# Hybrid encoder layer: the pooling products folded into the output weights on the chip, one pair of gates computed among the quads, and the weight sums begun later

## The chip, the cores and the metric

The kernel runs on one core of a Trainium2 chip. The metric is the device time of one execution in microseconds (us). The kernel before takes 2693.46 us (median of three runs, 2693.1 to 2695.12). Five engines work side by side: TensorE (PE) multiplies, VectorE (DVE) and ScalarE (ACT) do elementwise work, GpSimd (POOL) and SyncE (SP) here mainly issue transfers. Each executes its own instructions in program order and waits for the others by semaphores.

## The reference

One encoder layer on two requests of 256 and 1024 tokens (1280 in all), with 1024 channels, all in float32. What matters here is the mixing part:

```
z = rmsnorm(x) @ w_in                       # rq rk rv rg pin mq gl
gates = sigmoid(gl)                          # 3 x 1024 channels
# pooling branch, group gi of 256 channels, window w = 2, 4, 8, 16
mean = (cs[hi] - cs[lo]) / (hi - lo)         # centred window
d[gi] = mean - pin[gi]
y = einsum('bsgc,gcd->bsgd', d, pool_w) * pool_scale
y_pool = y @ w_pool_out
merged = gates[0]*y_ret + gates[1]*y_pool + gates[2]*y_mem
x = x + rmsnorm(merged @ w_o)
```

The other two branches are retention and attention over 256 memory tokens for each request, and a GeGLU network with 2 x 2816 inner columns follows. Between the differences `d` and `y_pool` there are only products with constants, so `pool_w`, `pool_scale` and `w_pool_out` can be multiplied with each other first.

## The kernel before

A float32 product is made of three matmuls (`mm3`, L161): each operand is split into a rounded high part and a low part, and high x high, high x low and low x high are added up. The high part is an ACT copy, the low part a DVE subtraction (`hilo`, L152; for weights `Weights.split`, L89 and L90). So every operand costs ACT and DVE time before PE can use it.

Weights come as units of 128 x 1024 (512 KB) in one fixed order. `Weights` keeps two raw tiles (`wr`, loaded by SP) and four split pairs (`wh`, `wl`). `take` hands units out and splits the next ones as soon as a pair is free; a load waits until the split of the unit two places before has freed its raw tile. A *gate unit* is one weight unit against all 1280 tokens: 24 matmuls for each of two groups of 512 tokens and one of 256, each followed by a sigmoid on ACT and a store by POOL.

`tick()` (L310) stands between groups of matmuls. It lets the weight ring take a step, issues `adding[0]` steps of the *weight sums*, and then advances each generator in the background list `bg` to its next `yield`. That is how the order of the work is set: nothing is rescheduled, the program order of the generators is the order on each engine.

The weight sums (`sums`, L201) are sums of weight quarters made by accumulating transfers of POOL through DRAM (five steps per pair of units: two copies on ACT's queue, then L214, L216, L218 and L220 on POOL's). They feed the *quads* (L611 on): a Strassen-like form for two weight units, in which 1024 of the tokens cost 84 matmuls of 512 columns in place of 96; the other 256 tokens take 48 matmuls of 256 columns in either form. The quads make `mq`, `pin` and `rg`, 12 in all, and take 229 to 527 us.

The stages of the first third are: memory keys and values (to 117 us; the values' group is `mem_v`, L523, and beside it x, loaded by POOL as `xr`, is normalised in the background, `x_stats`), the V projection (to 229), the quads, the memory stage (to 727), the pool stage (to about 915), the state and retention stages, and the merge that multiplies the three branches with their output weights.

In the memory stage PE multiplies K's rotary units (`rotary_unit`, L843 on) while `mem_chain` (L781 on) runs in the background: it loads K and V of a head, splits them (`khl`, `vhl`), and makes scores, softmax and outputs for 40 jobs. It yields three times before the first `split_k`. One gate unit follows.

In the pool stage PE multiplies nine gate units while two generators run. `pool_chain` (L901) takes the eight half groups m = 0 to 7 (two `pin` tiles, loaded by SP). For each it adds shifted copies on DVE (L939, L944; one add for window 2, four for window 16), mends the edges (L952, L955), forms the difference (L959), splits it on ACT and DVE (`dh`), and after two of them multiplies them with the split `pool_w` of the group (`pwh`) and stores the result (`ypo` on ACT, `yp_d`). `decay_matrix` (L461) makes four tables `dtab` for the retention: two DVE instructions for each (L467, L468), then a table load and four exponentials on ACT (L472), then four masks on DVE (L475).

Of the kernel before, what the change touches and what calls it, by code (L numbers as in the profile page):

```python
# [59 lines left out]
class Weights:  # L60
# [33 lines left out]
    def tick(self):  # L94
        self.load()
        self.split()
# [28 lines left out]
def encoder(ctx: ExitStack, tc: tile.TileContext, a: dict):  # L125
# [55 lines left out]
    def rsqrt_act(pool, v, between=None):  # L181
# [4 lines left out]
        if between:  # L186
# [9 lines left out]
             for k, o in (("mq", 40), ("pin", 32), ("rg", 24)) for i in range(H)]  # L196
# [46 lines left out]
    N_MEM, N_POOL = 1, 9  # L243
# [6 lines left out]
    gates = [w_in[48 + i] for i in range(24)]  # L250
    srcs += [w_in[8 + i] for i in range(8)] + gates[:N_MEM + N_POOL]
    srcs += [w_in[i] for i in range(8)] + gates[N_MEM + N_POOL:]
    srcs += [a["w_mem_out"][i] for i in range(8)]
    srcs += [a["w_pool_out"][i] for i in range(8)]
# [49 lines left out]
    def sum_step(n=1):  # L304
        for _ in range(n):
            next(summing, None)
# [194 lines left out]
    with tc.tile_pool(name="st0", bufs=2) as stp:  # L501
# [121 lines left out]
    with tc.tile_pool(name="quads", bufs=1) as qp:  # L623
# [25 lines left out]
        def emit(q, e, o, n, src, t=None):  # L649
            kind, i = quads[q][:2]  # L650
            if kind == "rg":
                y = t or qtile()
                s = qtile()
                nc.scalar.activation(s[:, 0:n], src, AF.Sigmoid)
                nc.vector.scalar_tensor_tensor(out=y[:, 0:n], in0=src, scalar=col("ret_gn", 2 * i + e), in1=s[:, 0:n],
                                               op0=ALU.mult, op1=ALU.mult)
                dst = g_d
            else:
                y = t
                if t is None:  # L660
                    y = qtile()
                    snap(y[:, 0:n], src)
                dst = mq_d if kind == "mq" else pin_d
            nc.gpsimd.dma_start(out=dst[i][:, e, o:o + n], in_=y[:, 0:n])
# [64 lines left out]
    def mem_chain():  # L729
# [83 lines left out]
        yield  # L813
        yield
        yield
# [49 lines left out]
    gate_n = [0]  # L865
# [36 lines left out]
    def pool_chain():  # L902
        pieces = ((PAD, 0, TP), (PAD + TP + PAD, TP, TS))
        pin = [pp.tile([P, PWA], F32, name=f"pin{i}") for i in range(2)]
        for t in pin:
            for s in (0, PAD + TP, PW - PAD):
                nc.gpsimd.memset(t[:, s:s + PAD], 0.0)

        def load(m):
            if m < 2 * len(WINDOWS):  # L910
                t = pin[m % 2]
                for s, o, n in pieces:
                    nc.sync.dma_start(out=t[:, s:s + n], in_=pin_d[m // 2][:, m % 2, o:o + n])

        load(0)
        load(1)

        def load_w(g):
            if g < len(WINDOWS):
                t = pwr[g] = pp.tile([P, 2, HD], F32, tag="pwr", name="pwr")  # L920
                nc.sync.dma_start(out=t, in_=a["pool_w"][:, g])

        pwr = {}
        load_w(0)
        yield
        for g, w in enumerate(WINDOWS):
            ph = pp.tile([P, 2, 2, HD], F32R, tag="pwh", name="pwh")
            hilo(pwr.pop(g)[:], ph[:, 0], ph[:, 1])
            load_w(g + 1)
            dh = []  # L930
            for c in range(2):
                x = pin[c]
                cur, lo, hi = x, PAD - 8, PW - PAD + 7
                step = 1
                while step < w:
                    t = pp.tile([P, PWA], F32, tag=f"ps{step in (2, 8)}", name="ps")
                    if step == 1:
                        lo += 1
                        nc.vector.tensor_tensor(out=t[:, lo:hi], in0=cur[:, lo - 1:hi - 1], in1=cur[:, lo:hi],  # L939
                                                op=ALU.add)  # L940
                    else:
                        k = step // 2
                        lo, hi = lo + k, hi - k
                        nc.vector.tensor_tensor(out=t[:, lo:hi], in0=cur[:, lo - k:hi - k],  # L944
                                                in1=cur[:, lo + k:hi + k], op=ALU.add)
                    cur = t
                    step *= 2
                    if step == 8:
                        yield
                for s, _, n in pieces:  # L950
                    e0 = cur[:, s:s + w // 2]
                    nc.vector.tensor_tensor(out=e0, in0=e0, in1=kcol(f"s{w}"), op=ALU.mult)  # L952
                    if w > 2:
                        e1 = cur[:, s + n - w // 2 + 1:s + n]
                        nc.vector.tensor_tensor(out=e1, in0=e1, in1=kcol(f"e{w}"), op=ALU.mult)  # L955
                    else:
                        e1 = cur[:, s + n - w // 2:s + n]
                r = cur[:, PAD:PW - PAD]
                nc.vector.scalar_tensor_tensor(out=r, in0=r, scalar=1.0 / w, in1=x[:, PAD:PW - PAD],  # L959
                                               op0=ALU.mult, op1=ALU.subtract)  # L960
                t = pp.tile([P, 2, PWA], F32R, tag="dh", name="dh", bufs=2)[:, :, 0:PCOLS]
                hilo(r, t[:, 0], t[:, 1])
                dh.append(t)
                yield
                load(2 * g + c + 2)
            yield
            for e in range(2):
                es = slice(e * P, (e + 1) * P)
                for s, o, n in ((0, 0, TP), (TP + PAD, TP, 512), (TP + PAD + 512, TP + 512, 512)):
                    b = chb(n)  # L970
                    for c in range(2):
# [5 lines left out]
                yield  # L977

    bg.append(pool_chain())
    bg.append(decay_matrix(pp))  # L980
    for _ in range(N_POOL):
        gate_unit(pp)
# [904 lines left out]
def _prepare(i, np):  # L1887
# [23 lines left out]
        "w_pool_out": _unit_fm(i["w_pool_out"][0], np),  # L1911
# [4 lines left out]
        "pool_w": i["pool_w"][0].reshape(4, 2, P, HD).transpose(2, 0, 1, 3),  # L1916
# [38 lines left out]
```

## Time and profile before

| what | value |
|---|---|
| median of three runs | 2693.46 us |
| the profiled execution, its span | 2693.02 us, 2691.0 us |
| PE busy | 2620.8 us, 97% |
| DVE, ACT, POOL busy | 53%, 36%, 12% |
| PE clock granted, mean | 0.986 |

PE is the engine that does nearly all of the span, so a stage gets shorter either by fewer matmul columns or by fewer waits of PE. A clock of 1.0 is 2.4 GHz; a stretch at half of it (1.2 GHz) shows as a clock below 1.0 in a window. A busy time of matmuls is modelled and each overlaps its neighbours, so the cost of one is read from the distance of two starts.

### The profile page before, as it was taken

What the parts mean: (1) busy time and instruction counts of PE and PEld (TensorE: products, weight loads), DVE (VectorE), ACT (ScalarE), POOL (GpSimd) and SP (SyncE); (2) the same over time, 40 slices, a digit from 0 to 9 for tenths busy, and PEclk for the clock granted to TensorE, in tenths of its full rate; (3) what the DMA queues carried; (4) which work ended last, traced back from release to release, by engine and by line L of the source; (5) the groups of instructions that cost most, each with busy time, mean ns of one, the idle gap of its engine ahead of it and who ended that gap; (6) DMA issues with size and microseconds to landing.
All of it is one profiled execution on the core that took longest, in us unless ns stands there. A gap on an engine that the chain in (4) does not pass through costs nothing.

```text
span 2691.0 us, 35137 instructions
## 1 busy us (share of the span) xinstructions
PE 2620.8 (97%) x13580; PEld 2240.8 (83%) x13580; DVE 1414.4 (53%) x2343; ACT 974.7 (36%) x1631; POOL 335.4 (12%) x507
## 2 busy tenths in 40 slices
PE   8899999999979899999999999998999999999998
PEld 6688888889958788888888888877888888888887
DVE  4542223466443465788633453557655666664554
ACT  5322223334332242333321120566444444444443
POOL 1111222212222222111100000010000000000000
PEclk9899999999989999999999999998999999999999
DMA  7986888877667787755344343453333333354443
GB/s 266 309 232 179 229 241 228 243 216 217 164 186 199 201 254 190 222 179 198 134 162 134 115 155 102 147 178 94 118 108 116 111 110 109 113 186 153 144 159 109
DMA packets 181429, 464.86 MB, mean 173 GB/s; under 512 B 20720, under 2 KB 48240, under 8 KB 180720
## 3 DMA queue, kind: packets, MB, share of 16 engines
q1 hardware_dynamic: 111072, 268.33, 30.3%
q0 software_dynamic: 54384, 146.83, 21.1%
q10 hardware_dynamic: 15808, 47.47, 5.5%
q8 instruction: 106, 1.74, 0.3%
q14 instruction: 59, 0.48, 0.1%
HBM read 360.58 MB, written 182.19 MB: 202 GB/s over the span
## 4 chain that ended last, share of the span: by engine, by line
PE 80%; issue 7%; DVE 5%; DMA 4%; ACT 2%; POOL 1%; SPq 0%; DVEq 0%; ACTq 0%; POOLq 0%
PE f L1521 15%; PE f L164 10%; PE f L163 9%; PE f L162 9%; PE mm L637 7%; PE mm L162 6%; PE mm L163 6%; PE mm L164 6%; PE ch L163 3%; PE ch L164 3%; PE ch L162 3%; PE ch L637 1%; DMA ypd<-ypo 1%; DVE ps L944 1%; DMA qkvr<-vd 1%
## 5 line engine op out<-in xcount | busy, mean ns | idle before, releaser
L90 DVE TENSOR_TENSOR wl<-wr,wh 128x1024 fp32r<-128x1024 f32 x268 | 327.4, 1223 | 493.7 <-ACT wh L89 488.7
L89 ACT ACTIVATE wh<-wr 128x1024 fp32r<-128x1024 f32 x268 | 280.7, 1051 | 282.0 <-PE f L163 156.5
L162 PE MATMUL mm<-b,wh 128*128 128x512 f32 (+1 forms) x960 | 342.8, 357 | 1.3 <-DVE rt L858 1.3
L163 PE MATMUL mm<-b,wh 128*128 128x512 f32 (+1 forms) x960 | 340.9, 355 | 0.0
L164 PE MATMUL mm<-b,wl 128*128 128x512 f32 (+1 forms) x960 | 340.5, 355 | 0.0
L1521 PE MATMUL f<-b,wh 128*128 128x512 f32 x880 | 274.4, 393 | 0.0
L162 PEld LDWEIGHTS mm<-b,wh 128*128 128x128 f32 x960 | 182.5, 190 | 25.8 <-DVE rt L858 1.8
L164 PEld LDWEIGHTS mm<-b,wl 128*128 128x128 f32 x960 | 182.1, 190 | 25.8
L163 PEld LDWEIGHTS mm<-b,wh 128*128 128x128 f32 x960 | 182.4, 190 | 23.6
L1521 PEld LDWEIGHTS f<-b,wh 128*128 128x128 f32 x880 | 162.3, 190 | 30.8
L1521 PE MATMUL f<-b,wl 128*128 128x512 f32 x440 | 172.0, 391 | 0.0
L163 PE MATMUL f<-b,wh 128*128 128x512 f32 (+1 forms) x432 | 153.4, 355 | 0.0
L162 PE MATMUL f<-b,wh 128*128 128x512 f32 (+1 forms) x432 | 153.2, 355 | 0.0
L164 PE MATMUL f<-b,wl 128*128 128x512 f32 (+1 forms) x432 | 152.8, 354 | 0.0
L164 PE MATMUL f<-wh,gl 128*128 128x512 f32 x390 | 151.8, 389 | 0.1
L162 PE MATMUL f<-wh,gl 128*128 128x512 f32 x390 | 151.7, 389 | 0.0
L163 PE MATMUL f<-wl,gl 128*128 128x512 f32 x390 | 151.7, 389 | 0.0
L155 DVE TENSOR_TENSOR gl<-b,gl 128x640 fp32r<-128x640 f32 x78 | 64.2, 824 | 118.3 <-ACT gl L154 118.2
L637 PE MATMUL mm<-T,wh 128*128 128x512 f32 x384 | 118.7, 391 | 0.0
L154 ACT ACTIVATE gl<-b 128x640 fp32r<-128x640 f32 x78 | 57.5, 740 | 153.7 <-PE f L164 153.7
L1521 PE MATMUL f<-hc,wh 128*128 128x512 f32 x352 | 108.9, 391 | 0.0
L162 PE MATMUL f<-h2p,wh 128*128 128x256 f32 x352 | 100.4, 285 | 3.2 <-ACT h2p L154 3.2
(383 smaller groups left out, 5919.6 us busy)
## 6 DMA issues: line engine op xcount, KB each, us to landing
wr<-w_in_in SPq DMA_DIRECT2D x72, 512.0 KB, 5.9
wr<-w_up_in SPq DMA_DIRECT2D x44, 512.0 KB, 3.5
wr<-w_down_in SPq DMA_DIRECT2D x44, 512.0 KB, 3.5
wr<-s12d SPq DMA_DIRECT2D x34, 512.0 KB, 3.6
wr<-s34d SPq DMA_DIRECT2D x34, 512.0 KB, 3.6
b<-fgd SPq DMA_DIRECT2D x44, 320.0 KB, 5.1
h2s<-gtd SPq DMA_DIRECT2D x48, 256.0 KB, 3.8
s12d<-w_up_in ACTq DMA_DIRECT2D x22, 512.0 KB, 5.8
```

Of the source, the lines that this page charges most:

```text
L89: self.nc.scalar.activation(h, r[:], AF.Copy)
L90: self.nc.vector.tensor_tensor(out=l, in0=r[:], in1=h.bitcast(F32), op=ALU.subtract)
L154: nc.scalar.activation(hi, src, AF.Copy)
L155: nc.vector.tensor_tensor(out=lo, in0=src, in1=hi.bitcast(F32), op=ALU.subtract)
L162: nc.tensor.matmul(out, ah, bh, start=first, stop=False)
L163: nc.tensor.matmul(out, ah, bl, start=False, stop=False)
L164: nc.tensor.matmul(out, al, bh, start=False, stop=last)
L637: nc.tensor.matmul(b, w[x][:, ks], in_term(nm, c, y), start=first and c == k == 0, stop=last and c == 3 and k == 2, skip_group_check=True)
L944: nc.vector.tensor_tensor(out=t[:, lo:hi], in0=cur[:, lo - k:hi - k], in1=cur[:, lo + k:hi + k], op=ALU.add)
L1521: nc.tensor.matmul(b, w[x][:, ks], hterm(nm, c, y), start=first and c == k == 0, stop=last and c == 3 and k == 2, skip_group_check=True)
```

## The change

It has five parts.

1. The quads get a thirteenth kind `gate`, made of gate units 0 and 1 (`NG = 2`); `emit` applies the sigmoid and writes to `gate_d`.
2. The memory stage has two gate units in place of one, and the pool stage 2 + 1 + 2 + 1 = 6 in place of 9. With the two in the quads the number before the state stage stays ten.
3. `pool_chain` no longer splits the differences nor multiplies: POOL stores them to `yp_d` as they are. In their place `fold(g)` multiplies the transposed `pool_w` of group g, scaled by `pool_scale` in its split (`fold_split`), with two weight units of `w_pool_out` from the ring: four blocks of 512 columns, each of two products of three matmuls, so 24 matmuls. The result goes to DRAM (`wp_d`) by ACT and POOL and is read as the merge's pooling weights. `pool_wT` (1 MB) comes in one load on SP. `decay_matrix` is now ahead of `pool_chain` in `bg`.
4. In `tick` the sums' step comes after the background generators, and `adding[0] = 1` is set when the first `mem_v` runs, three ticks later than before. There are 35 sums in place of 34.
5. `mem_chain` yields four times in place of three before `split_k(0)`.

```
-             for k, o in (("mq", 40), ("pin", 32), ("rg", 24)) for i in range(H)]
+             for k, o in (("mq", 40), ("pin", 32), ("rg", 24)) for i in range(H)] + [("gate", 0, w_in[48], w_in[49])]
-    N_MEM, N_POOL = 1, 9
+    NG, N_MEM, N_FOLD = 2, 2, (2, 1, 2, 1)
...
+    gates = [w_in[48 + i] for i in range(NG, 24)]
+    wp_d = dram.tile([P, KC, KC, P], F32, name="wpd")
+    srcs += [w_in[8 + i] for i in range(8)] + gates[:N_MEM]
+    gates = gates[N_MEM:]
+    for g in range(len(WINDOWS)):
+        srcs += [a["w_pool_out"][2 * g], a["w_pool_out"][2 * g + 1]] + gates[:N_FOLD[g]]
+        gates = gates[N_FOLD[g]:]
-    srcs += [a["w_pool_out"][i] for i in range(8)]
+    srcs += [wp_d[:, i].rearrange("p a b -> p (a b)") for i in range(KC)]
...
     def tick(step=True):
         ws.tick()
-        sum_step(adding[0])
         for g in list(bg) if step else ():
...
+        sum_step(adding[0])
...
         def mem_v(p, j, b):
+            adding[0] = 1
...
-        adding[0] = 1
         token_major(8, memT, 4, mem_v)
...
+            elif kind == "gate":
+                y = t or qtile()
+                nc.scalar.activation(y[:, 0:n], src, AF.Sigmoid)
+                dst = gate_d[2 * i + e]
...
-        yield
-        yield
-        yield
+        for _ in range(4):
+            yield
         split_k(0)
...
-                t = pp.tile([P, 2, PWA], F32R, tag="dh", name="dh", bufs=2)[:, :, 0:PCOLS]
-                hilo(r, t[:, 0], t[:, 1])
...
-            for e in range(2):
-                es = slice(e * P, (e + 1) * P)
-                for s, o, n in ((0, 0, TP), (TP + PAD, TP, 512), (TP + PAD + 512, TP + 512, 512)):
-                    b = chb(n)
-                    for c in range(2):
-                        mm3(b, ph[:, 0, c, es], ph[:, 1, c, es], dh[c][:, 0, s:s + n], dh[c][:, 1, s:s + n],
-                            c == 0, c == 1)
-                    y = pp.tile([P, 512], F32, tag="ypo", name="ypo", bufs=2)
-                    nc.scalar.activation(y[:, 0:n], b, AF.Copy, scale=col("pool_scale", 2 * g + e))
-                    nc.gpsimd.dma_start(out=yp_d[g][:, e, o:o + n], in_=y[:, 0:n])
+            for s, o, n in pieces:
+                nc.gpsimd.dma_start(out=yp_d[m // 2][:, m % 2, o:o + n], in_=cur[:, s:s + n])
             yield
+            load(m + 2)
+    bg.append(decay_matrix(pp))
     bg.append(pool_chain())
-    bg.append(decay_matrix(pp))
-    for _ in range(N_POOL):
-        gate_unit(pp)
+    pwr = pp.tile([P, 4, 2, HD], F32, name="pwr")
+    nc.sync.dma_start(out=pwr, in_=a["pool_wT"])
+    pw = pp.tile([P, 2, 4, 2, HD], F32R, name="pw")
+    def fold_split(g):
+        for d in range(2):
+            hilo(pwr[:, g, d], pw[:, 0, g, d], pw[:, 1, g, d], col("pool_scale", 2 * g + d))
+    def fold(g):
+        rows = ws.take(2)
+        for c in range(2):
+            cs = slice(c * P, (c + 1) * P)
+            for f in range(2):
+                b = chb(512)
+                fs = slice(f * 512, (f + 1) * 512)
+                for d in range(2):
+                    mm3(b, pw[:, 0, g, d, cs], pw[:, 1, g, d, cs], rows[d][0][:, fs], rows[d][1][:, fs],
+                        d == 0, d == 1)
+                o = pp.tile([P, 512], F32, tag="wpo", name="wpo", bufs=4)
+                nc.scalar.activation(o, b, AF.Copy)
+                nc.gpsimd.dma_start(out=wp_d[:, 4 * f:4 * f + 4, 2 * g + c, :],
+                                    in_=o[:].rearrange("p (a b) -> p a b", b=P))
+    for g in range(len(WINDOWS)):
+        fold_split(g)
+        fold(g)
+        tick()
+        for _ in range(N_FOLD[g]):
+            gate_unit(pp)
```

On DVE, just before the second product group of the pool stage, the kernel before has the following (`pwh` is the low part of that group's `pool_w`, `wl` that of a weight unit, the last two rows are the first adds of half group m = 2):

```order
L468 SCALAR_TENSOR_TENSOR dtab<-rel,lg,dtab 128x512
L90 TENSOR_TENSOR wl<-wr,wh 128x1024
L155 TENSOR_TENSOR pwh<-pwr,pwh 128x512
L939 TENSOR_TENSOR ps<-pin_6191 128x1310
L944 TENSOR_TENSOR ps<-ps 128x1308
```

and the changed kernel, just before the second fold (`pw` is the low part of the second group's `pool_w`; the first row is the difference of m = 3, the three adds are those of m = 4):

```order
L952 SCALAR_TENSOR_TENSOR ps<-ps,pin_6500 128x1296
L480 TENSOR_SCALAR dtab<-dtab 128x512 x4
L934 TENSOR_TENSOR ps<-pin_6499 128x1310
L939 TENSOR_TENSOR ps<-ps 128x1308
L939 TENSOR_TENSOR ps<-ps 128x1304
L158 SCALAR_TENSOR_TENSOR pw<-pwr,pk,pw 128x256 x2
L90 TENSOR_TENSOR wl<-wr,wh 128x1024
```

Before, `pwh` stood ahead of its group's adds, and the differences of m = 2 and m = 3 behind it were what the products waited for; now no product needs a difference, but `pw` stands behind m = 2, m = 3, the four masks of `dtab` and the adds of m = 4. On ACT the exponentials of `dtab` with a table load on either side stand in both kernels in the last gate unit ahead of this place; now the copy of the second `pool_w` is the next but one after them.

At the start of the memory stage DVE has, in the kernel before (`khl`, `qhl` and `vhl` are the low parts of the memory's keys, queries and values, `rot` a rotated K, `mx` the first maximum of the softmax):

```order
L860 TENSOR_TENSOR rot<-rt_4306,rt_4307 128x2x256
L155 TENSOR_TENSOR khl<-kraw,khl 128x1024
L155 TENSOR_TENSOR qhl<-qraw,qhl 128x512
L155 TENSOR_TENSOR vhl<-vraw,vhl 128x1024
L777 TENSOR_REDUCE mx<-ch 128x2
```

and in the changed one, with the third group (256 columns) of the rotary unit in between:

```order
L868 TENSOR_TENSOR rot<-rt_4500,rt_4501 128x2x256
L155 TENSOR_TENSOR khl<-kraw,khl 128x1024
L155 TENSOR_TENSOR qhl<-qraw,qhl 128x512
L866 TENSOR_TENSOR rt_4573<-mm,cos 128x256
L867 TENSOR_TENSOR rt_4574<-mm,sin 128x256
L868 TENSOR_TENSOR rot<-rt_4573,rt_4574 128x256
L866 TENSOR_TENSOR rt_4573<-mm,sin 128x256
L867 TENSOR_TENSOR rt_4574<-mm,cos 128x256
L868 TENSOR_TENSOR rot<-rt_4573,rt_4574 128x256
L155 TENSOR_TENSOR vhl<-vraw,vhl 128x1024
L786 TENSOR_REDUCE mx<-ch 128x2
```

The keys' split keeps its place behind the same rotation, while the first maximum, and so the first scores on PE, come one group of matmuls later.

POOL's loads of the transposed input `xT`, which is normalised in the background of the memory values, stand among the first sums before:

```order
L371 DMA xr<-xT_in 128x1280 x5
L214 DMA s12d_71<-w_in_in 256x1x512
L371 DMA xr<-xT_in 128x1280 x2
L214 DMA s12d_72<-w_in_in 256x1x512
L371 DMA xr<-xT_in 128x1280
L216 DMA s34d_105<-w_in_in 128x512
```

and ahead of all of them after:

```order
L376 DMA xr<-xT_in 128x1280 x8
L214 DMA s12d_71<-w_in_in 256x1x512
L214 DMA s12d_72<-w_in_in 256x1x512
L216 DMA s34d_106<-w_in_in 128x512
L214 DMA s12d_73<-w_in_in 256x1x512
```

No load of `xT` is now behind a sum.

## Rows read from the trace of the kernel before

**Rows 1.** The page's busy time of each engine, share and instructions, whole span.

```profile
PE 2620.8 (97%) x13580; PEld 2240.8 (83%) x13580; DVE 1414.4 (53%) x2343; ACT 974.7 (36%) x1631; POOL 335.4 (12%) x507
```

**Rows 2.** Busy us by stretch: start:end, length, engines, granted clock, DMA share, GB/s.

```profile
230.00:530.00 300.00, 300.00 (x1592) 259.35 (x1591) 96.92 (x107) 91.81 (x133) 84.07 (x118) 1.00 0.84 228
530.00:570.00 40.00, 35.25 (x178) 30.38 (x177) 18.81 (x32) 8.62 (x16) 8.38 (x11) 0.91 0.92 254
...
752.00:908.00 156.00, 128.47 (x625) 108.07 (x626) 71.75 (x84) 47.92 (x71) 43.03 (x65) 0.89 0.68 178
```

**Rows 3.** Chain of waits in a quad: start, us, what.

```profile
240.07 0.12 PE ch L162
...
241.50 5.47 PE mm L637 x24
```

**Rows 4.** Waits of PE, pool stage (724 to 908): us, times, longest.

```profile
PE ch L162 <- ACT dh L154: 22.6, 5, 7.4
PE ch L163 <- DVE dh L155: 5.1, 5, 1.2
```

**Rows 5.** Busy us by stretch around the second wait of the pool stage.

```profile
758.00:765.00 7.00, 2.19 (x6) 1.71 (x7) 5.50 (x8) 3.67 (x5) 2.42 (x4) 0.50 0.41 68
765.00:772.00 7.00, 7.00 (x39) 6.13 (x38) 2.95 (x5) 0.81 (x2) 1.68 (x3) 0.77 0.95 257
```

**Rows 6.** Groups by line and form, pool stage: busy, mean ns | idle before.

```profile
L90 DVE TENSOR_TENSOR wl<-wr,wh 128x1024 fp32r<-128x1024 f32 x9 | 11.0, 1222 | 67.6 <-ACT wh L89 67.6
...
L975 ACT ACTIVATE ypo<-ch,pk 128x512 f32<-128x512 f32 x15 | 10.3, 688 | 46.0 <-DMA ypd<-ypo 38.6 <-PE ch L164 7.3
L869 ACT ACTIVATE gate<-mm 128x512 f32<-128x512 f32 x17 | 10.0, 591 | 14.4 <-PE mm L164 13.7 <-ACT wh L89 0.6
L89 ACT ACTIVATE wh<-wr 128x1024 fp32r<-128x1024 f32 x9 | 9.5, 1053 | 0.0
...
L468 DVE SCALAR_TENSOR_TENSOR dtab<-rel,lg,dtab 128x512 f32<-128x512 f32 x4 | 3.0, 751 | 0.1
...
L467 DVE TENSOR_SCALAR dtab<-rel,lg 128x512 f32<-128x512 f32 x4 | 2.0, 488 | 0.0
L475 DVE TENSOR_SCALAR dtab<-dtab 128x512 f32<-128x512 f32 x4 | 1.4, 417 | 0.0
```

**Rows 7.** DVE's timeline, first and last instruction of one half group, window 4.

```profile
788.53 1.52 DVE L939 TENSOR_TENSOR ps<-pin 128x1310 f32<-128x1310 f32 x1
...
792.04 1.51 DVE L959 SCALAR_TENSOR_TENSOR ps<-ps,pin 128x1296 f32<-128x1296 f32 x1
```

**Rows 8.** ACT's timeline at the decay tables' exponentials.

```profile
780.41 1.28 ACT L472 ACT_TABLE_LOAD   x1
781.70 2.19 ACT L472 ACTIVATE dtab<-dtab 128x512 f32<-128x512 f32 x4
```

**Rows 9.** Landing of the tiles pin, then pwr (min/median/max), whole span.

```profile
DMA to landing us min/median/max: 2.1/5.3/7.9
DMA to landing us min/median/max: 3.0/5.8/8.7
```

**Rows 10.** DMA issues of the pool stage: the table of distances.

```profile
rel<-rel_in SPq DMA_DIRECT2D x1, 512.0 KB, 10.4
```

**Rows 11.** Waits of PE, 60 to 130 us.

```profile
PE mm L162 <- ACT sv L525: 9.8, 2, 5.3
```

**Rows 12.** Chain of waits from 100 to 118 us.

```profile
100.93 12.59 DMA xr<-xT_in
```

**Rows 13.** DVE's timeline at that load's landing.

```profile
113.54 1.49 DVE L415 TENSOR_TENSOR xr<-xr,xrb 128x1280 f32<-128x1280 f32 x1 [2.71 <-DMA xr<-xT_in]
```

**Rows 14.** Waits of PE, 530 to 570 us.

```profile
PE ch L163 <- DVE khl L155: 3.4, 1, 3.4
```

**Rows 15.** DVE's timeline at the end of that wait.

```profile
556.01 1.22 DVE L155 TENSOR_TENSOR khl<-kraw,khl 128x1024 fp32r<-128x1024 f32 x1
```

More of the change, by code (lines that the diff above doesn't have):

```diff
@@ L662, in emit @@
                     snap(y[:, 0:n], src)
-                dst = mq_d if kind == "mq" else pin_d
-            nc.gpsimd.dma_start(out=dst[i][:, e, o:o + n], in_=y[:, 0:n])
+                dst = (mq_d if kind == "mq" else pin_d)[i][:, e]
+            nc.gpsimd.dma_start(out=dst[:, o:o + n], in_=y[:, 0:n])
         def close(q, e, o, op, x, y):
@@ L863, in rotary_unit @@
             tick()
-    gate_n = [0]
+    gate_n = [NG]
     def gate_out(m, pool, o, n, b):
@@ L909, in load @@
         def load(m):
-            if m < 2 * len(WINDOWS):
-                t = pin[m % 2]
+            if m < KC:
                 for s, o, n in pieces:
-                    nc.sync.dma_start(out=t[:, s:s + n], in_=pin_d[m // 2][:, m % 2, o:o + n])
+                    nc.sync.dma_start(out=pin[m % 2][:, s:s + n], in_=pin_d[m // 2][:, m % 2, o:o + n])
         load(0)
         load(1)
[L918 to L921, printed above, removed]
@@ L979, in encoder @@
-    bg.append(pool_chain())
-    bg.append(decay_matrix(pp))
-    for _ in range(N_POOL):
-        gate_unit(pp)
+        yield
+        yield
+        for m in range(KC):
+            w, x = WINDOWS[m // 2], pin[m % 2]
+            cur, lo, hi = x, PAD - 8, PW - PAD + 7
+            step = 1
+            while step < w:
+                t = pp.tile([P, PWA], F32, tag="ps", name="ps", bufs=4)
+                if step == 1:
+                    lo += 1
+                    nc.vector.tensor_tensor(out=t[:, lo:hi], in0=cur[:, lo - 1:hi - 1], in1=cur[:, lo:hi],
+                                            op=ALU.add)
+                else:
+                    k = step // 2
+                    lo, hi = lo + k, hi - k
+                    nc.vector.tensor_tensor(out=t[:, lo:hi], in0=cur[:, lo - k:hi - k],
+                                            in1=cur[:, lo + k:hi + k], op=ALU.add)
+                cur = t
+                step *= 2
+                if step == 8:
+                    yield
+            for s, _, n in pieces:
+                e0 = cur[:, s:s + w // 2]
+                nc.vector.tensor_tensor(out=e0, in0=e0, in1=kcol(f"s{w}"), op=ALU.mult)
+                if w > 2:
+                    e1 = cur[:, s + n - w // 2 + 1:s + n]
+                    nc.vector.tensor_tensor(out=e1, in0=e1, in1=kcol(f"e{w}"), op=ALU.mult)
+            r = cur[:, PAD:PW - PAD]
+            nc.vector.scalar_tensor_tensor(out=r, in0=r, scalar=1.0 / w, in1=x[:, PAD:PW - PAD],
+                                           op0=ALU.mult, op1=ALU.subtract)
+            for s, o, n in pieces:
+                nc.gpsimd.dma_start(out=yp_d[m // 2][:, m % 2, o:o + n], in_=cur[:, s:s + n])
+            yield
+            load(m + 2)
@@ L1910, in _prepare @@
         "w_ret_out": _unit_fm(i["w_ret_out"][0], np),
-        "w_pool_out": _unit_fm(i["w_pool_out"][0], np),
+        "w_pool_out": i["w_pool_out"][0].reshape(KC, P, D),
         "w_mem_out": _unit_fm(i["w_mem_out"][0], np),
@@ L1915, in _prepare @@
         "w_down": dn,
-        "pool_w": i["pool_w"][0].reshape(4, 2, P, HD).transpose(2, 0, 1, 3),
+        "pool_wT": i["pool_w"][0].transpose(0, 2, 1).reshape(4, 2, P, HD).transpose(2, 0, 1, 3),
         "pk": pk,
```

47 lines of the change are left out of this document (2 added, 45 removed).

## The prediction

> **What bounds the kernel now.** I began with the busy times: PE works 2620.8 of 2691.0 us [rows 1]. So at most 70 us can be won by mending waits, and the rest only by fewer matmul columns. Next I read the windows. In the quads PE is busy 300.00 of 300 us, while ACT and DVE do less than 100 each: nothing but columns counts there. The pool stage from 752 to 908 is the loosest stretch: PE is busy 128.47 of 156 us at a granted clock of 0.89 [rows 2]. Its waits name the cause: five times PE waits for ACT's copy of a difference and five times for DVE's low part, 22.6 + 5.1 = 27.7 us together [rows 4]. A clock of 0.89 means that 0.22 x 156 = 34 us were spent at the half level (1.2 GHz); what PE did in them I come to below. Two shorter waits are touched as well: for ACT's `sv` in the memory values (9.8 us in two, the longer 5.3) [rows 11], and for `khl` at the start of the memory stage, 3.4 us [rows 14]. Durations are those of one execution of 2693.02 us (span 2691.0, so 2.0 around it); the median is 0.44 higher.
>
> **Pitch.** 24 matmuls of 512 columns take 5.47 us, 0.228 each; one of 256 takes 0.12 [rows 3].
>
> **The gate pair among the quads.** Two gate units cost 96 x 0.228 + 48 x 0.12 = 27.6 us. As a quad they keep the 48 and have 84 of the 96, so 12 x 0.228 = **2.7 us** go. The quad adds a sigmoid in place of a copy, four stores on POOL, and two more summed units. ACT is busy 92 of 300 us, DVE 97 and POOL 84 there [rows 2], so I take nothing for them. Transfers are the cover that could go: the DMA share is 0.84 there, yet no quad of the twelve waited. One unit that comes late would cost up to a landing, 5.3 us by `pin`'s median [rows 9]. The third gate unit that leaves the pool stage is multiplied in the memory stage, at the same price.
>
> **Products.** Before: four groups, two output blocks, two inner blocks, three matmuls each for pieces of 512, 512 and 256 columns, so 96 matmuls of 512 and 48 of 256. The folds: four of 24, so 96 of 512. The 48 of 256 go: 48 x 0.12 = **5.7 us**. This and the 2.7 do not depend on any wait.
>
> **Waits of the pool stage.** ACT loses eight `dh` and four `pwh` copies and 24 `ypo`, and gains eight weight copies (1.05) and 16 `wpo` (about 0.69); DVE loses eight `dh` and gains eight weight subtractions (1.22) [rows 6]. So the engines' load is about even, and what matters is what stands in front of each fold. I add up each engine's queue from the last gate unit ahead of a fold.
>
> - First fold: it needs `pw`, whose 1 MB is asked for some 5.4 us of PE work ahead. No row has 1 MB; 256 KB of the same kind took 3.0, 5.8 and 8.7 us, least, median, most [rows 9]. I take about 8 and, with the two splits (under 0.59 each on ACT by the 512-column gate, about 0.4 each on DVE, half of the 0.75 of a 512-column one [rows 6]), a wait of **3.5 us**; ends 2 (ACT's own queue) and 6.
> - Second fold, by DVE's order: after the gate unit's first group come its sigmoid 0.59, `wh` 1.05 and `wl` 1.22 (2.9), a table row pair 0.49 + 0.75, then half groups m = 2 and 3. One of these takes from 788.53 to 793.55, 5.0 us [rows 7]. Then four masks of 0.42 (1.7), three adds of m = 4 at 1.52 (4.6), and `pw` 0.4: 2.9 + 1.2 + 10.0 + 1.7 + 4.6 + 0.4 = 20.8 us. PE has the unit's other two groups in the meantime, 24 x 0.228 + 24 x 0.12 = 8.3. Wait **12.4 us**. ACT would be late by 3.4 anyway: a table load of 1.28 and the exponentials' 2.19 [rows 8], a second load, sigmoid and copy, after PE's second group.
> - Third: 2.9, then m = 5 (three adds 4.6, edges and difference 1.9), three adds of m = 6 (4.6) and `pw` 0.4, together 14.4, less 8.3: **6.1 us**.
> - Fourth: two gate units lie ahead, **1.0 us**.
>
> Together 23.0 against 27.7: **4.7 us** less. This supposes that `pin` lands in its median of 5.3 us [rows 9], which hides behind the other half group (5.0 us). At the longest, 7.9, the sum is 29; without the first fold's wait and with the second at ACT's 3.4 it is some 10 to 17. Ends: 17 and 32. The stores of differences on POOL replace those of `ypo`, and nobody reads them before the merge; the 512-byte pieces of `wp_d` likewise, hundreds of us ahead.
>
> **Clock.** Between 758 and 765 us all was at half level, but PE was busy only 2.19 us; from 765 to 772, at 0.77, it worked all the time with 3.2 us at half, which costs 1.6 [rows 5]. With the few slow matmuls before that, one such stretch costs about 2 us, and the three of the stage about 6. The waits of 12.4, 6.1 and 3.5 may well bring three again, so I take 0, with ends -6 and +4. The Trainium skill ("TensorE: Matmul & The Clock Gate", section "HAM oscillation — how this bites in real kernels") puts the extra time at half of the throttled time. That would be 17 us for the 34 here, and a stage without waits would gain 11 us more than by my rows; the trace disagrees, since PE stood idle in most of that time and cannot be slowed there.
>
> **Sums begun later.** The last `xT` load was issued at 100.93 and landed after 12.59 us [rows 12]; DVE stood 2.71 us for it [rows 13], and its result is ahead of `sv` on ACT. Now it is ahead of all sums on POOL. I expect it to land at least 2.7 us sooner, so the wait of 5.3 shrinks to 2.7: **2.6 us**. Ends: 0 (the tile it loads into comes free no sooner) and 5.3. The other wait is in front of the first sum, and I leave it.
>
> **Memory stage.** The scores come one group (24 x 0.12 = 2.9 us) later, while `khl` is behind the same rotation and ends at 556.01 + 1.22 = 557.23 [rows 15]. So the wait shrinks from 3.4 to about 1.0, less than the 2.9 since the job that waits in front of it on ACT moves a little: **2.4 us**. At 0.91 of 40 us some 7.2 us were at half level [rows 2]; nearly all of it followed that wait, with PE at work, and costs up to half, 3.3. I take it as gone: **5.7 us** together, ends 0 and 6.7.
>
> **Sum.** 2.7 + 5.7 + 4.7 + 2.6 + 5.7 = 21.4. 2693.0 - 21.4 = 2671.6, and 0.4 more for the median: **2672 us**. Of this 8.4 is columns, the rest waits.
>
> **Rivals.**
>
> *A, the pool stage's waits go nearly all.* DVE would have to be ahead of the order I added up, so that ACT's 3.4, the first fold's 2 and small ones remain, 6 in place of 23, and the clock's 6 come back: 2672 - 17 - 6 = 2649 us. For it: DVE is busy only 72 of 156 us in the stage [rows 2]. Against: the masks and adds stand ahead of `pw` in order, whatever DVE's share. By the Trainium skill's rule above this rival would end near 2638, which no row supports.
>
> *B, slow transfers, and no gain early.* With `pin` at 7.9 and 1 MB at 11 the waits are 32, 9 more, and the 8.3 of the memory values and the memory stage fail: 2672 + 17 = 2689 us. For it: there is a new 1 MB load and the weight units of `w_pool_out` in the same stretch. Against: nine weight units before, fourteen loads of a like size now, but four `pool_w` loads fewer.
>
> *C, the half groups' loads set the pace; slower.* DVE waits in order for `pin`, and `pw` and `wl` stand behind it. `pin` is asked for when the difference two half groups earlier has been formed, with 5 us of DVE work in between. If loads land 14 us after their issue, each of the three pairs m = 2 to 7 shows 8 to 9 us, about 25 more, and `xT` gains nothing: 2672 + 25 + 2.6 = 2699.6 us. For it: in this stage `rel` took 10.4 us [rows 10], and `xT` 12.59. It decides against the change from a landing of some 14 us on. Against: no `pin` took more than 7.9.
>
> *D, sums begun later do nothing.* `xT` is held by its tile's release, and the 2.6 fall away: 2674.5, inside the likeliest's range.
>
> **Chances.** The likeliest (with D) 0.65, with its own range 2662 to 2682; A 0.13; B 0.15; C 0.07. From 2652 to 2690 some 0.8 is held: the likeliest, most of B, a little of A. Below 0.2% (5.4 us) a measurement of this kernel can't tell a change, so faster means under 2688.1 and slower over 2698.8: faster is the likeliest, A and a third of B, 0.83; C's greater part is slower, 0.06; 0.11 is left for the same.
>
> **What would show it.** Of the profile after: PE at 300 of 300 in the quads with 13 of them, the end of the thirteenth 24.9 us behind the twelfth's; PE waiting for `pw` at four places, longest at the second fold with DVE named; no wait for `dh`; `khl` about 1 us at the memory stage's start and a clock of 1.0 there; the longer `sv` wait at 2.7. It is wrong if the second fold starts without a wait (A), if DVE idles on `pin` for more than 5 us a time (C), or if later stages, whose instructions don't change, lose what was won.

## The result, and the profile after

The changed kernel takes 2671.64 us (median of four runs, 2668.98 to 2675.04) beside 2693.28 of the kernel before: ratio 0.9919, 95% interval 0.9902 to 0.9936. The forecast was 2672. The profiled execution took 2672.97 us with a span of 2671.1, so against the 2693.02 and 2691.0 of before some 20 us went. The sum came out, but the terms under it did not all; they are taken up below.

The page's busy times, beside those of [rows 1]:

```profile
PE 2602.4 (97%) x13520; PEld 2225.3 (83%) x13520; DVE 1418.4 (53%) x2352; ACT 975.8 (37%) x1634; POOL 346.4 (13%) x519
```

PE is busy 18.4 us less, and idle 1.5 us less. Of the 18.4 the columns are 8.4; much of the rest is half clock, for the mean granted clock rose from 0.986 to 0.991, which over the span is some 27 us less at half clock.

The windows of the changed kernel (start:end, length, busy us of PE, weight loads, DVE, ACT, POOL, granted clock, DMA share, GB/s): the quads, the start of the memory stage, the pool stage. They answer to [rows 2]:

```profile
230.00:555.00 325.00, 325.00 (x1717) 280.69 (x1716) 104.69 (x115) 99.98 (x145) 92.97 (x131) 1.00 0.84 231
550.00:590.00 40.00, 39.73 (x210) 34.01 (x210) 21.14 (x36) 10.64 (x19) 7.93 (x10) 1.00 1.01 286
742.00:884.00 142.00, 112.81 (x535) 93.98 (x534) 69.60 (x89) 40.59 (x63) 48.40 (x75) 0.89 0.91 260
```

Thirteen quads run as the twelve did, without an idle moment. The memory stage's start has 0.27 us of idle time in 40 in place of 4.75, and the full clock in place of 0.91. The pool stage is as loose as before: 29.2 us idle at a clock of 0.89.

PE's only wait from 550 to 600 us, where [rows 14] had 3.4 us for `khl`:

```profile
PE ch L801 <- DVE pr L793: 0.3, 1, 0.3
```

The wait for `sv` ahead of the V projection, before and after (PE's timeline, with the idle time ahead in brackets), then POOL's issue of the last `xT` load in the changed kernel, then that load's time to landing, before and after:

```profile
117.05 0.80 PE L162 MATMUL mm<-wh,b 128*128 128x512 f32 x1 [5.33 <-ACT sv L525]
114.72 0.50 PE L162 MATMUL mm<-wh,b 128*128 128x512 f32 x1 [3.01 <-ACT sv L531]
101.28 0.53 POOL L376 DMA_DIRECT2D xr<-xT_in  x1 [3.47 <-DVE b L158]
xr<-xT_in POOLq DMA_DIRECT2D x1, 640.0 KB, 12.6
xr<-xT_in POOLq DMA_DIRECT2D x1, 640.0 KB, 8.7
```

The wait fell from 5.33 to 3.01 us, near the 2.7 foretold. The other wait for `sv`, which I had left alone, went from 4.5 to 4.7 us and is now the longer.

PE's waits in the pool stage, where [rows 4] had the two for `dh`:

```profile
PE ch L164 <- DVE pw L158: 20.3, 2, 13.3
PE ch L162 <- ACT pw L157: 8.9, 4, 3.6
```

The waits for a difference are gone, and in their place PE waits for the split `pool_w` of the next fold: at the first fold 3.6 us, at the second 3.5 for ACT and 13.3 for DVE, at the third 0.9 and 7.0, at the fourth 0.9, together 29.2 against 27.7.

The table takes both profiled executions apart at the same events, counted from PE's first matmul: the quads' first matmul on the sum term T2, their last on T4, the last product with the memory values, the first product of a state's keys and values. "Excess" is the length less the matmuls at their pitch (0.228 for 512 columns, 0.12 for 256, half of that for 128), so waits and half clock together. The 5.7 us of the third row from below are the 48 matmuls at their pitch, counted and not timed, so the row under it is what remains of the stage.

| stretch | before | after | work moved | gained | forecast |
|---|---|---|---|---|---|
| to the quads | 235.83 | 232.26 | 0 | 3.6 | 2.6 (sums later) |
| quads | 289.97 | 314.85 | +24.88, for 27.6 of two gate units | 2.7 | 2.7 |
| memory stage, excess | 13.1 | 6.5 | | 6.6 | 5.7 |
| pool stage, 48 matmuls of 256 | | | -5.7 | 5.7 | 5.7 |
| pool stage, excess | 37.7 | 36.2 | | 1.5 | 4.7 |
| all that follows | 1752.2 | 1752.5 | 0 | -0.2 | 0 |

Together 19.9.

### The profile page after: what moved, and what is told of

It reads as the page before. It is cut to its first block, busy times and chain, and to the rows that moved or that the text cites. A ratio compares the mean times of both kernels' runs of the same rounds, so it can differ in the third digit from the quotient of the medians.

```text
span 2671.1 us, 35093 instructions
## 1 busy us (share of the span) xinstructions
PE 2602.4 (97%) x13520; PEld 2225.3 (83%) x13520; DVE 1418.4 (53%) x2352; ACT 975.8 (37%) x1634; POOL 346.4 (13%) x519
## 4 chain that ended last, share of the span: by engine, by line
PE 88%; DVE 4%; DMA 3%; ACT 2%; issue 2%; SPq 0%; POOL 0%; ACTq 0%; DVEq 0%; POOLq 0%
PE f L1528 15%; PE f L164 11%; PE f L162 10%; PE f L163 10%; PE mm L642 8%; PE mm L162 7%; PE mm L163 7%; PE mm L164 7%; PE ch L164 4%; PE ch L163 4%; PE ch L162 3%; PE ch L642 1%; DMA wr<-w_kv_in 1%; DMA pin<-pind 1%; DVE wl L90 1%
## 5 line engine op out<-in xcount | busy, mean ns | idle before, releaser
L90 DVE TENSOR_TENSOR wl<-wr,wh 128x1024 fp32r<-128x1024 f32 x278 | 339.7, 1224 | 490.2 <-ACT wh L89 485.3
L89 ACT ACTIVATE wh<-wr 128x1024 fp32r<-128x1024 f32 x278 | 291.2, 1051 | 272.2 <-PE f L163 151.8
L162 PE MATMUL mm<-b,wh 128*128 128x512 f32 (+1 forms) x912 | 324.8, 356 | 0.0
L163 PE MATMUL mm<-b,wh 128*128 128x512 f32 (+1 forms) x912 | 323.3, 354 | 0.0
L164 PE MATMUL mm<-b,wl 128*128 128x512 f32 (+1 forms) x912 | 322.8, 354 | 0.0
L164 PEld LDWEIGHTS mm<-b,wl 128*128 128x128 f32 x912 | 172.3, 189 | 24.3
L162 PEld LDWEIGHTS mm<-b,wh 128*128 128x128 f32 x912 | 172.6, 189 | 22.8
L163 PEld LDWEIGHTS mm<-b,wh 128*128 128x128 f32 x912 | 172.6, 189 | 22.3
L1528 PEld LDWEIGHTS f<-b,wh 128*128 128x128 f32 x880 | 161.9, 189 | 30.7
L642 PE MATMUL mm<-T,wh 128*128 128x512 f32 x416 | 128.7, 391 | 0.0
```

Of the source, the lines that this page charges most:

```text
L89: self.nc.scalar.activation(h, r[:], AF.Copy)
L90: self.nc.vector.tensor_tensor(out=l, in0=r[:], in1=h.bitcast(F32), op=ALU.subtract)
L162: nc.tensor.matmul(out, ah, bh, start=first, stop=False)
L163: nc.tensor.matmul(out, ah, bl, start=False, stop=False)
L164: nc.tensor.matmul(out, al, bh, start=False, stop=last)
L642: nc.tensor.matmul(b, w[x][:, ks], in_term(nm, c, y), start=first and c == k == 0, stop=last and c == 3 and k == 2, skip_group_check=True)
```

## The experiments

Each variant was run four or five times, e6 eleven times; a ratio is to the kernel before on the same chip, with its 95% interval. The edits are against the changed kernel unless something else is said. The changed kernel's own is 0.9919.

**Sums early again (e1).** Both halves of part 4 are taken back.

```
-        sum_step(adding[0])        # behind the background generators
+        sum_step(adding[0])        # ahead of them
...
-            adding[0] = 1          # in mem_v
+        adding[0] = 1              # ahead of token_major(8, memT, 4, mem_v)
```

> Theory (the order on POOL counts): with the sums' steps ahead of the background again and begun with the first memory value, the longer wait for ACT's sv is 5.3 us again instead of 3.0, the quads start at 228.9 us instead of 225.3, and the time is 2671.6 + 3.6 = 2675 us. Rival (the xT loads wait for their tile's release in any case): sv stays at 3.0, the quads start within 0.5 us of 225.3, the time stays at 2671 to 2672.

2683.65 us, ratio 0.9959 (0.9946 to 0.9971): 0.0040 above the changed kernel, some 11 us, three times what the theory gave. The wait it spoke of came back as forecast:

```profile
PE mm L162 <- ACT sv L530: 9.5, 2, 5.6
```

5.6 us, and the quads began 4.1 us later. But 4.1 is not 11 (in its profile the memory stage is 2.3 us longer too, and the pool stage 4.7), so the halves were run apart, and part 4 alone in the kernel before.

**Only the order (e5), only the begin (e6).**

> Only the order inside tick is as before: the sums' step ahead of the background generators; it is still begun with the first memory value. Both halves together (e1) cost some 10 us against the changed kernel. Theory (the order counts, in every tick up to 1100 us, since the sums' issues on ACT and POOL stand ahead of the background's work): ratio to the kernel before 0.995 to 0.996 as in e1, and the memory and pool stages longer by 2 and 4 us, as there. Rival (the begin counts): 0.992, the memory and pool stages within 1 us of the changed kernel's 193.1 and 177.0.

> Only the begin is as before: adding[0] = 1 ahead of the memory values, the sums' step still behind the background. Theory (the order counts): ratio to the kernel before 0.992 to 0.993, the start to the quads at most 3 us longer than 232.3. Rival (the begin counts): 0.995 to 0.996, the quads begin some 4 us later and the later stages lose as in e1.

The order alone does not change the time: 2672.93 us, 0.9922 (0.9908 to 0.9936). Its rival's stage lengths are not met, though: in the one profile the memory stage is 2.1 us longer and the pool stage 1.9 shorter. The early begin alone costs most: 2691.55 us over eleven runs, 0.9989 (0.998 to 0.9998), some 19 us over the changed kernel. So the theory that the order counts has fallen, and the begin counts, more than the rival's 0.996 at most, and more than when it is combined with the old order. One place of the extra loss shows: in this run's V projection PE waits for ACT's `vst`, and ACT has behind it a split whose input, `xs`, was late. Waits of PE, then the chain of waits (start, us, what), then DVE's timeline:

```profile
PE mm L162 <- ACT sv L530: 9.7, 2, 5.6
PE mm L162 <- ACT vst L619: 7.1, 1, 7.1
```

```profile
153.76 13.29 DMA xs<-xT_in
```

```profile
163.64 1.28 DVE L593 SCALAR_TENSOR_TENSOR xs<-xs,pk,xrb 128x1024 f32<-128x1024 f32 x1 [4.84 <-DMA xs<-xT_in]
167.16 1.28 DVE L593 SCALAR_TENSOR_TENSOR xs<-xs,pk,xrb 128x1024 f32<-128x1024 f32 x1 [2.23 <-DMA xs<-xT_in]
```

A load of `xs` took 13.29 us while sums ran; DVE stood 4.84 and 2.23 us for two of them, ACT's splits stood behind DVE, and PE lost 7.1 us and worked on at half clock (0.43 us from one matmul of 512 columns to the next, in place of 0.228).

**The later begin in the kernel before (e11).** Part 4 alone, on the kernel before.

> The kernel before with part 4 alone: the sums' step behind the background generators and begun with the first memory value. Theory (the begin is worth as much as in the changed kernel, where taking it back cost some 10 us): ratio 0.995 to 0.997. Rival (it is worth the wait for sv that I had added up, 2.6 us, or 3.6 by the start of the quads): 0.9985 to 0.999, with the quads' start at 225 to 226 us in place of 228.9.

2681.36 us, 0.9954 (0.9942 to 0.9967), as the theory had it: this part alone gives 12 us, where the whole change gives 22. In its profile the stretch to the quads takes 229.0 us, 6.8 less than before, the memory stage is 4.2 us shorter although it still yields three times, and the pool stage 5.3. (These are more than 12 together: the profiled execution took 2677.26 us, the least of the five.) Its waits at the memory stage's start, where [rows 14] had 3.4 us, and the window, which had 0.91 in [rows 2]:

```profile
PE ch L163 <- DVE khl L155: 1.7, 1, 1.7
PE ch L792 <- DVE pr L784: 1.1, 1, 1.1
```

```profile
540.00:580.00 40.00, 36.99 (x230) 32.95 (x229) 28.00 (x53) 14.13 (x31) 9.23 (x12) 1.00 0.84 225
```

The wait for `khl` is halved and the clock full without the fourth yield. That the first stretch is shorter is no accident of one profile: with the late begin it is 228.5 to 232.3 us in all eleven profiles here, the changed kernel's own being near the upper end, and with the early one 235.8, 236.4 and 244.0.

**Three yields (e2).**

```
-        for _ in range(4):
+        for _ in range(3):
             yield
         split_k(0)
```

> Theory (the fourth yield covers khl): with three yields PE waits 3.4 us for khl again at the start of the memory stage, a stretch of 6.8 us at half clock follows it, and the time is 2671.6 + 3.4 + 3.4 = 2678 us; the 1.35 us wait for the rotary's rt comes back or not. Rival (the quad of gates at the end of the quads, which needs ACT in place of DVE, has freed DVE early enough): no wait of more than 0.5 us, no half clock, 2671 to 2672 us.

2677.89 us, 0.9934 (0.992 to 0.9947), which is 4 us above the changed kernel by the ratios, with intervals that overlap. The waits and the window of its memory stage's start:

```profile
PE ch L163 <- DVE khl L155: 1.7, 1, 1.7
```

```profile
550.00:590.00 40.00, 38.08 (x201) 33.05 (x200) 21.25 (x37) 10.15 (x18) 7.09 (x9) 0.96 0.95 278
```

The wait is 1.7 us, not 3.4, and the half clock 3.4 us long, not 6.8: the memory stage's excess is 9.0 in place of 6.5. So the fourth yield is worth 2.5 us here; the rest of the 6.6 is the sums'.

**No quad of gates (e3).** `NG, N_MEM = 0, 4`, and the quads without the entry `gate`.

> Gate units 0 and 1 are multiplied as two gate units at the end of the memory stage in place of a thirteenth quad. Theory (12 matmuls of 512 columns, nothing else): the quads end 24.9 us earlier, the memory stage is 27.6 us longer, the time 2671.6 + 2.7 = 2674.3 us. Rival (one weight sum and two unit loads fewer relieve the transfers of the pool stage or of the quads' end): less than 1 us of difference, or faster.

2674.1 us, 0.9925 (0.9912 to 0.9937). The difference from the changed kernel, 0.0006 or 1.6 us, agrees with 2.7 but cannot be told from none. The stage length tells it: its twelve quads take 289.97 us between the two events as before, the thirteen 314.85, and 24.88 is 2.7 less than the 27.6 that two gate units cost at the pitch. The two units themselves are not in the memory stage of the table but behind its last event: e3's pool stage is 26.2 us longer, waits included.

**Splits first (e4).** The second to fourth `pw` are split behind the first fold.

```
+    fold_split(0)
     for g in range(len(WINDOWS)):
-        fold_split(g)
         fold(g)
+        if g == 0:
+            for k in range(1, len(WINDOWS)):
+                fold_split(k)
         tick()
```

> The pw of groups 1 to 3 are split right after the first fold instead of just before their own. Theory (PE waits at the second and third fold for pw alone, which stands on DVE behind half groups and masks): the waits of 16.7 and 8.0 us go to under 2 each, with them some 10 us at half clock while PE works; the pool stage's waits fall from 29.2 to 5 to 8 us, the time to 2645 to 2652 us. Rival (the split weights wl of the same folds stand behind the same half groups on DVE): PE waits for wl instead, 8 to 13 us at the second fold or the unit behind it, and the time is 2660 to 2668 us.

2659.1 us, 0.9865 (0.9852 to 0.9879). It lies between the theory's range and the rival's, close to the latter; its ratio is 0.0054 below the changed kernel's, some 15 us. The waits of PE:

```profile
PE ch L1015 <- DMA k<-kd: 4.5, 1, 4.5
PE ch L162 <- ACT pw L157: 3.4, 1, 3.4
PE mm L164 <- DVE wl L90: 3.0, 2, 2.4
PE ch L163 <- DVE wl L90: 2.0, 1, 2.0
```

The waits for `pw` at the later folds are gone, with 13.2 us left of 29.2, and the half clock of the stage fell from 30.7 to 13.7 us. But `wl` is waited for in three places, and a new wait of 4.5 us stands at the state stage's start: with PE sooner there, its keys are not.

**Three `pin` tiles (e7).** `load(m + 3)` into three tiles; for room `PWA = 1328` and `wpo` with three buffers.

> Three pin tiles in place of two, so a half group is asked for one half group earlier; to make room the tiles are 1328 wide in place of 1408 and wpo has three buffers in place of four. Theory (my sum for the second and third fold was short by DVE's waits for pin, 5.6 and 2.5 us, which came from a load that stood behind a raw weight load on SP and landed late): these two waits of DVE go, PE's waits at the second fold fall from 16.7 to 11 to 12.4 and at the third from 8.0 to 5.5 to 6.1, the time by 6 to 8 us, ratio 0.989 to 0.990. Rival (the loads only crowd each other, the landing gets longer): DVE's wait for pin stays over 3 us, the waits of PE within 2 us of what they were, ratio 0.991 to 0.993.

2664.5 us, 0.9888 (0.9873 to 0.9903), at the edge of the theory's range. PE's waits:

```profile
PE ch L164 <- DVE pw L158: 12.0, 2, 7.6
PE ch L162 <- ACT pw L157: 8.5, 4, 3.5
```

DVE has no wait for `pin` left in the stage. The second fold waits 3.5 + 7.6 = 11.0 us and the third 0.9 + 4.4 = 5.3: with the loads out of the way the queue arithmetic of the prediction (12.4 and 6.1) holds to 1.4 and 0.8 us.

**Gates first (e8).** In each group the gate units come before the fold (the weight order with them), and all of `pw` is split behind the first gate unit.

```
     for g in range(len(WINDOWS)):
-        fold_split(g)
+        for k in range(N_FOLD[g]):
+            gate_unit(pp)
+            if g == k == 0:
+                for j in range(len(WINDOWS)):
+                    fold_split(j)
         fold(g)
         tick()
-        for _ in range(N_FOLD[g]):
-            gate_unit(pp)
```

> In each group the gate units come ahead of the fold, and all pw are split behind the first gate unit. Theory (then the 1 MB load lands under a gate unit and pw is never late): against the variant with early splits (ratio 0.9865) the first fold's wait of 3.4 goes, and 4.5 at the state stage's start for k changes little: ratio 0.984 to 0.986. Rival (the last fold now stands right ahead of the state stage, whose tables and keys have less cover): the wait there grows from 4.5 to 8 or more and eats what the first fold gives: 0.9865 to 0.989.

2650.49 us, 0.9839 (0.9826 to 0.9853): at the lower edge of the theory's range, the fastest here, 0.0080 below the changed kernel. The first fold waits no more, and the wait at the state stage's start did not grow. What is left:

```profile
PE ch L163 <- DVE wl L90: 8.3, 2, 6.2
PE ch L1014 <- DMA k<-kd: 3.0, 1, 3.0
```

**Gates first with three `pin` tiles (e9), then with sums later still (e10).** e9 joins e7 and e8; e10 also sets `adding[0] = 1` ahead of the V projection in place of `mem_v`.

> The gate units ahead of the folds with early splits of pw (ratio 0.984 alone), and three pin tiles as in the run with those alone (0.989). Theory (what is left at the second fold, 2.1 and 6.2 us for wl, is DVE standing for pin with wl behind it): these waits fall to under 3 us together, the pool stage from 155.4 to 147 to 150 us, ratio 0.981 to 0.983. Rival (it is DVE's sheer work in that place): the waits stay over 6, ratio 0.9835 to 0.985.

> The run before, and the sums begun still later, at the V projection's start in place of the first memory value. Theory (while the sums run, their transfers crowd the loads of the memory stage's input): the stretch to the quads is 2 to 4 us shorter, ratio lower by 0.001 than the run before. Rival (nothing crowds there any more, and now the sums crowd the x loads of the V projection or come too late for the first quads): the same ratio or up to 0.004 higher, with a wait in the V projection or at the quads' start.

e9 takes 2664.99 us, 0.9894 (0.9878 to 0.9909): two edits that each help are together 0.0055 worse than the one. The longest of PE's waits, ACT's timeline ahead of the second fold and the chain of waits there (`wpd` is the fold results' place in DRAM):

```profile
PE ch L162 <- ACT wh L89: 15.1, 2, 12.9
```

```profile
790.03 1.55 ACT L980 ACTIVATE wpo<-ch 128x512 f32<-128x512 f32 x3
811.86 0.60 ACT L980 ACTIVATE wpo<-ch 128x512 f32<-128x512 f32 x1 [20.28 <-DMA wpd<-wpo]
812.36 1.05 ACT L89 ACTIVATE wh<-wr 128x1024 fp32r<-128x1024 f32 x1
```

```profile
800.92 10.84 DMA wpd<-wpo
```

ACT had copied three results of the first fold and stood 20.28 us for the fourth, which needs the first's buffer. That buffer's store was issued by POOL only at 800.9, behind the two stores of a difference that DVE formed at 798.6, and took 10.84 us. The weight's high part `wh`, which the second fold needs, stands behind that copy on ACT. PE also waited 9.2 us at the state stage's start for its keys. So I suspected the `wpo` buffer, given away for room, and not the third `pin` tile; e12 tests it. Neither theory nor rival had named it. e10 has the same stand and the same time, 2664.36 us, 0.9896 (0.988 to 0.9911), so a begin still later gives nothing that can be told.

**One ring for gates and results (e12).** As e9, but in the pool stage `wpo` and `gate` share six buffers.

```
-                o = pp.tile([P, 512], F32, tag="wpo", name="wpo", bufs=3)
+                o = pp.tile([P, 512], F32, tag="gate", name="wpo", bufs=6)
```

> As the run with gates ahead and three pin tiles (0.9894), the order on every engine unchanged, but gates and fold results share one ring of six buffers in place of three each. Theory (there ACT stood 20.3 us at the fourth wpo copy, for a buffer whose store was held on POOL behind the stores of the differences, and wh, a weight load on SP and the keys of the state stage stood behind it): that stand goes, PE's wait of 12.9 at the second fold falls under 3 and the 9.2 at the state stage's start to 3 or less, ratio 0.978 to 0.983. Rival (the third pin tile moves SP's loads so that weight units come late in any case): 0.986 or more, with PE waiting for wh again.

2651.47 us, 0.9846 (0.9833 to 0.986). ACT's stand was the cause: 13 us come back, with the third `pin` tile still there. But the ratio is above the range that I gave, and level with e8, so the third tile gives nothing that can be told here. PE's waits:

```profile
PE ch L163 <- DVE wl L90: 4.6, 1, 4.6
PE ch L1017 <- DMA k<-kd: 4.1, 1, 4.1
```

Both are above the 3 us that the theory allowed each. 8.7 us are left in place of e8's 11.3, which five runs cannot tell apart.

## Why the prediction was right, and where it was not

**The sum.** Forecast were 21.4 us; the profiles show 19.9. The pool stage's excess gave 3.2 less than forecast, the first stretch and the memory stage 1.0 and 0.9 more, and what follows lost 0.2. That the time was met to 0.4 us is luck in part: errors of both signs cancel, and the four runs alone lie 6 us apart.

**Columns.** The 2.7 came out to a tenth by the quads' length. The 5.7 is the count of matmuls at their pitch; no stage length and no run isolates it.

**Pool stage: the step "second fold, by DVE's order" failed.** PE's waits were to fall from 27.7 to 23.0 us and grew to 29.2. The price of each instruction was right; the first fold waited 3.6 (3.5 foretold) and the fourth 0.9 (1.0), and the 1 MB landed in 8.0 us. What failed is the supposition under the sum, that `pin` lands in 5.3 us and hides behind the other half group. DVE's timeline of the changed kernel, with the idle time ahead of an instruction in brackets:

```profile
783.45 1.51 DVE L952 SCALAR_TENSOR_TENSOR ps<-ps,pin 128x1296 f32<-128x1296 f32 x1
...
793.37 1.51 DVE L952 SCALAR_TENSOR_TENSOR ps<-ps,pin 128x1296 f32<-128x1296 f32 x1
800.48 1.52 DVE L934 TENSOR_TENSOR ps<-pin 128x1310 f32<-128x1310 f32 x1 [5.60 <-DMA pin<-pind]
...
811.35 0.88 DVE L158 SCALAR_TENSOR_TENSOR pw<-pwr,pk,pw 128x256 fp32r<-128x256 f32 x2
...
835.96 1.52 DVE L934 TENSOR_TENSOR ps<-pin 128x1310 f32<-128x1310 f32 x1 [2.52 <-DMA pin<-pind]
```

and SP's, the weight load ahead of the `pin` loads:

```profile
788.78 0.33 SPq L73 DMA_DIRECT2D wr<-w_pool_out_in  x1
789.21 17.12 SPq L920 DMA_DIRECT2D pin<-pind  x6
```

The difference of m = 1 was formed at 784.96. Its tile could have been loaded again from there, but on SP the load stands behind a raw weight load that waits for a `wl` (ended 788.76), and so it (the first two of the six issues) was issued at 789.2 and landed at 800.3. DVE stood 5.60 us with `pw` behind it, and 2.52 us ahead of the third fold. That is rival C's mechanism, at a smaller price; of the signs that I had named, C's, more than 5 us of DVE on `pin` at a time, was met once. Landings of `pin` now are

```profile
DMA to landing us min/median/max: 2.1/7.3/10.6
```

against 7.9 at most in [rows 9]. Of the step's error of 6.2 us (29.2 for 23.0) 4.3 lie at the second fold and 1.9 at the third; e7, which makes the loads early, took 5.7 and 2.7 off there, more than the error, so the sum itself was 1.4 and 0.8 us too high.

**Clock.** Half-clock time in the pool stage was 34.1 us before and 30.7 after, again in three stretches. The excess less the waits, which is what the clock and everything else cost, was 10.0 us before and is 7.0 now: 3.0 gained where I took 0. With the waits 1.5 us longer that makes the table's 1.5. The Trainium skill ("TensorE: Matmul & The Clock Gate", section "HAM oscillation — how this bites in real kernels") counts half of the throttled time, which would be an estimated 15.4; as before, the trace disagrees for a stage in which PE stood for most of that time. The longest of the three stretches, with PE busy 3.74 of 17 us at a clock of 0.50:

```profile
798.00:815.00 17.00, 3.74 (x9) 2.48 (x8) 14.32 (x22) 1.52 (x2) 3.76 (x6) 0.50 0.74 210
```

**Sums: the step "sums begun later" was mis-sized.** I priced the one wait for `sv` at 2.6 us, and it fell by 2.3, but not by the way that I gave. The last `xT` load was issued no sooner: at 101.28 us in place of 100.93, with POOL standing 3.47 us until DVE had read the tile. It landed after 8.7 us in place of 12.6. With the order alone taken back (e5) it took 8.6 us, with the begin alone (e6) 10.6, with both (e1) 12.3, so in these profiles its time goes with the begin of the sums and not with its place on POOL. In the two profiles the first stretch gained 3.6; by e11 the part alone is worth 12 us in the kernel before, and by e1 some 11 in the changed one. It reaches further than the wait that I looked at: the memory stage gained from it too. Of the 6.6 us where I had given 5.7 wholly to the fourth yield, e2 leaves 2.5 to the yield and 4 to the sums, and e11's memory stage, with three yields, gained 4.2. With the yield kept and the sums early (e1) the memory stage lost only 2.3, so the shares depend on which is taken first. So two terms were near in size and wrong in cause. Rival D's condition held, that the load waits for its tile's release, but not its consequence, that the begin does nothing.

**Rivals.** A, with the waits nearly gone and 2649 us, is not what the change did, but e8 comes to that time: 2650.5, with all `pw` split early and the gate units ahead. B's failing early gains did not come; C is above.

**Open.** No run takes the fold (parts 2 and 3) back alone, so its worth is known only from the table's count and remainder. Why the pool stage, 600 us after the sums began, is 5.3 us shorter in e11 and 4.7 longer in e1, and why the early begin costs 8 us more with the new order (e6) than with the old (e1), is settled by no run: in the one profile of each, e6's first stretch is 7.6 us longer (244.0 and 236.4), and its 7.1 us wait behind `xs` is in it. That the sums slow other transfers is the likeliest reason and is not shown beyond the loads named here. The pool stage's excess also differed without a change to its order (34.3 in e5, 36.2 in the changed kernel).

## What to carry to other kernels

A queue sum by program order foretold the waits of the first and fourth folds to 0.1 us, and the other two to 1.4 and 0.8 once the loads were out of the way (e7), but only then: date every transfer in it too. Look for what stands ahead of the load on its own issuing engine, and do not take the median landing for a load that moves into a busier stretch: here the pool stage's DMA share went from 0.68 to 0.91, and `pin`'s median from 5.3 to 7.3 us. Split constants that a later product needs early, not in front of the product and behind the background work (e4, 15 us). When room is made by dropping a buffer, ask which in-order engine will stand for it: here, with the gate units first, a ring of three for `wpo` cost 13 us, and gave them back when six buffers were shared; in e7's order ACT stood at most 3.6 us for the same ring of three.

## What the runs showed that I had not expected

Moving the begin of a background stream of transfers by three ticks changed the time by 11 to 19 us (e1 and e11 with the order in `tick`, e6 without it), more than all the matmul columns that the change saves (8.4). And in eight profiles with the same program up to the quads (the changed kernel, e2 to e4, e7 to e9, e12) the stretch to there took 228.5 to 232.3 us: this spread of 4 us is as large as several of the terms in the sum, so a term read from one pair of profiles is good to no better than that.
